# Experts ranked by token count on chip, the twelve emptiest run as six fp32 pairs, overflow only in a loop

## The chip, the cores and the metric

One core of a Trainium2 chip runs the whole program in one launch. The metric is the device time of that launch in microseconds. TensorE (PE) multiplies matrices, VectorE (DVE), ScalarE (ACT) and GpSimd (POOL) work element by element, SyncE (SP) mostly issues transfers, and 16 DMA engines move data. Each engine follows its own order of instructions and waits on semaphores for the others.

## The reference

Two layers over 1024 tokens of width 1024. Each has a mixer (layer 0 a state space scan, layer 1 dilated window attention) and then a mixture of 32 experts. The change touches the experts alone:

```python
def _hierarchical_moe(x, w_rg, b_rg, w_re, b_re, w_gate, w_up, w_down):
    ...
    g_w, g_idx = lax.top_k(jax.nn.softmax(g_logits, axis=-1), 1)      # one of 4 groups
    ...
    e_w, e_idx = lax.top_k(jax.nn.softmax(e_logits, axis=-1), MOE_TOP_K)  # 2 of its 8 experts
    e_w = e_w / jnp.sum(e_w, -1, keepdims=True)
    gates = (g_w * e_w).reshape(-1)
    ...
        h = jax.nn.silu(xb @ w_gate[e]) * (xb @ w_up[e])              # hidden width 512
        return h @ w_down[e]
    ...
    y = jax.ops.segment_sum(y_rows * row_gate[:, None], row_tok, num_segments=t + 1)[:t]
...
        x = _layer_norm(DEEPNORM_ALPHA * x + ffn, ln_g[i, 1], ln_b[i, 1])
```

Everything is float32. Each token goes to two experts, so a layer has 2048 assignments, 64 an expert on average. An expert's three matrices are 6 MB, and all 32 of them 192 MB a layer.

## The kernel before

**Tokens.** A router (class `Router`) works out gates and, for each expert, a column of token numbers `toks` with 112 places (`CAP`). Rows of x lie in the DRAM tensor X. `gather` (L924) brings an expert's rows into a buffer G by an indirect DMA on POOL's queue; places without a token are out of bounds and move nothing. `rows_out` (L997 to L999) copies the result to y and adds it to the DRAM tensor S with an indirect scatter. S starts as a copy of X (L1063) and holds the sum that the layer's norm reads at the end.

**Steps.** `Moe.run` walks 33 steps: the 32 experts in order, and a step 32 put in after the first 12 (`OVER`). That step takes the rows beyond 112 of the first expert that has too many; `overflow` (called at step 4) finds it, `place` lists its rows, and its weights are loaded only if there is one (`cond`). PE does that step either way. A loop at the very end takes further overflows, if any.

**Inside a step.** Step n does `up` for expert n (gate and up products into the PSUM tiles gu), the transposes of the next rows (L940), and `down` for expert n-1 (into dn), then the transposes of h. TensorE runs single-pass fp32r products, so weights and rows are split into a high part and a low rest, and every product is three matmuls (`mm3`, L175 to L177). ACT makes the high part wh (L916) and DVE the rest wl (L920) of each weight piece.

**Weights.** An expert's weights come in six pieces of 1 MB, four for gate and up and two for down. SP issues them in order (L900). They land in a ring of 10 buffers `wr`, and the first 14 pieces use four more buffers (`pre`). A buffer is free again once both splits have read it, so SP waits for the splits. The order of loads, splits, transposes and matmuls on each engine is as written in `Moe.run` (`chain`, `behind`); the rest follows from waits on tiles.

Of the kernel before, what the change touches and what calls it, by code (L numbers as in the profile page):

```python
# [21 lines left out]
P = 128  # L22
# [20 lines left out]
OVER = 12  # L43
# [7 lines left out]
OVT = 4  # L51
# [10 lines left out]
YB = 3  # L62
PLD = 6
# [579 lines left out]
class Router:  # L643
# [5 lines left out]
    def __init__(self, tc, cm, pool, keep, early, dram, layer, runs, w_rg, b_rg, w_re, b_re):  # L649
# [14 lines left out]
        self.X = dram.tile([T, D], F32, name=f"X{layer}")  # L664
        self.known = pool.tile([P, NT, 2, 2], F32, name=f"known{layer}")
# [11 lines left out]
    def tile(self, i, a, half, pt, pl):  # L677
# [4 lines left out]
        (nc.scalar if self.layer in XACT else nc.sync).dma_start(token_rows(self.X, self.runs[i], D), a)  # L682
# [147 lines left out]
    def overflow(self, pool, tmp, pp):  # L830

        nc, cm, V = self.nc, self.cm, self.nc.vector
        pc = pp([32, 2])
        nc.tensor.matmul(pc[:, 0:1], lhsT=self.total, rhs=cm.ones_b[:, 0:1], start=True, stop=True)
        ex, gt, M = tmp[:32, 0:1], tmp[:32, 64:64 + T // CAP], tmp[:32, 128:129 + 2 * OV]
        V.tensor_scalar(gt, cm.iota[0:32, 1:T // CAP + 1], float(CAP), None, op0=ALU.mult)
        V.tensor_tensor(gt, gt, pc[:, 0:1].to_broadcast([32, T // CAP]), op=ALU.is_lt)
        V.tensor_reduce(ex, gt, axis=AX.X, op=ALU.add)
        pc2 = pp([32, 2])
        nc.tensor.matmul(pc2[:, 0:1], lhsT=cm.triu[0:32, 0:32], rhs=ex, start=True, stop=True)  # L840
        V.tensor_tensor(M[:, 0:OV], cm.iota[0:32, 0:OV], pc2[:, 0:1].to_broadcast([32, OV]), op=ALU.is_ge)
        V.tensor_tensor(M[:, OV:2 * OV], M[:, 0:OV], ex.to_broadcast([32, OV]), op=ALU.mult)
        V.tensor_copy(M[:, 2 * OV:], ex)
        pr = pp([P, 2 * OV + 1])
        nc.tensor.matmul(pr, lhsT=cm.ones[0:32, :], rhs=M, start=True, stop=True)
        tab = pool.tile([P, OV + 2], I32, name="ov_tab", bufs=1)
        V.tensor_scalar(tab[:, 0:OV], pr[:, 0:OV], 31.0, None, op0=ALU.min)
        V.tensor_copy(tab[:, OV:OV + 1], pr[:, 2 * OV:])
        V.tensor_scalar(tab[:, OV + 1:], pr[:, 2 * OV:], 1.0, 0.0, op0=ALU.subtract, op1=ALU.max)

        base = pool.tile([P, OV], F32, name="ov_base", bufs=1)
        V.scalar_tensor_tensor(base, pr[:, OV:2 * OV], -1.0, cm.iota[:, 1:OV + 1], op0=ALU.mult, op1=ALU.add)
        V.tensor_scalar(base, base, float(CAP), None, op0=ALU.mult)
        V.scalar_tensor_tensor(base, pr[:, 0:OV], 1024.0, base, op0=ALU.mult, op1=ALU.add)
        return tab, base
# [8 lines left out]
class Moe:  # L864
# [6 lines left out]
    def run(self, extra=lambda tmp: None):  # L871
# [5 lines left out]
        dr = self.scope.enter_context(tc.tile_pool(name=f"m_dram{self.layer}", bufs=1, space=DRAM))  # L877
# [12 lines left out]
        self.S = S = dr.tile([T, D], F32, name="S")  # L890
# [4 lines left out]
        def raw(src, wr=None, **kw):  # L895
            wr = wr or spare()
            if kw:
                nc.gpsimd.memset(wr, 0.0)
            with behind(tc, *self.loads[-1:]):
                self.loads.append(nc.sync.dma_start(wr.rearrange("p (k n) -> p k n", n=src.shape[-1]), src, **kw))  # L900
            return wr
# [8 lines left out]
        def weights(src, wr, *gate):  # L910

            cnt[0] += 1
            n = src.shape[-1]
            wh = hp.tile([P, 2048], F32R, name="wh")
            wl = lp.tile([P, 2048], F32R, name="wl")
            chain("act", lambda: nc.scalar.activation(wh, wr, AF.Copy))  # L916
            if cnt[0] in PLO:
                nc.gpsimd.tensor_tensor(wl, wr, wh.bitcast(F32), op=ALU.subtract)
            else:
                chain("dve", lambda: nc.vector.tensor_tensor(wl, wr, wh.bitcast(F32), op=ALU.subtract), *gate)  # L920
            return [(wh[:, k:k + n], wl[:, k:k + n]) for k in range(0, 2048, n)]

        def gather(g, tok):
            return nc.gpsimd.indirect_dma_start(out=g[:CAP], out_offset=None, in_=rt.X[:, :],  # L924
                                         in_offset=bass.IndirectOffsetOnAxis(ap=tok[:CAP], axis=0),
                                         bounds_check=T - 1, oob_is_err=False)

        def parts(wg, wu, wd):

            up = [w.rearrange("(p k) n -> p k n", k=KD)[:, q:q + 4, :] for w in (wg, wu) for q in range(0, KD, 4)]  # L930
            down = [wd.rearrange("(k p) n -> p k n", p=P)[:, q:q + 2, :] for q in range(0, 4, 2)]
            return list(zip(up, [None] * len(up))), list(zip(down, [None] * len(down)))

        def flip(src, width):

            pts = []
            for q in range(0, width, 4):
                pts.append(ps.tile([P, 4, CAP], F32, name="tr"))
                for k in range(4):
                    make = lambda: nc.tensor.transpose(pts[-1][:, k, :], src[q + k], cm.ident[:CAP, :CAP])  # L940
# [4 lines left out]
        def parted(pts, name):  # L945
            h, l = [sp.tile([P, 4 * len(pts), CAP], F32R, name=name + x, bufs=XB) for x in "hl"]
# [6 lines left out]
        def rows_in(g):  # L953
            g = g[:CAP].rearrange("t (p k) -> t k p", k=KD)
            return parted(flip([g[:, k, :] for k in range(KD)], KD), "x")

        def up(x, pieces, between=lambda: None):

            xh, xl = x
            pg = [ps.tile([CAP, 512], F32, name="gu") for _ in range(2)]  # L960
            n = 0
            for j, (src, wr) in enumerate(pieces):
                for w in wr if isinstance(wr, list) else weights(src, wr):
                    i, kk = divmod(n, KD)
                    make = lambda: mm3(nc, pg[i], xh[:, kk, :], xl[:, kk, :], *w, kk == 0, kk == KD - 1)
                    last = make() if n else chain("pe", make)
                    n += 1
                if j == BETW:
                    between()
# [3 lines left out]
        def hidden(pg, gate):  # L973

            h = sp.tile([P, 512], F32, name="h")[:CAP]
            chain("act", lambda: nc.scalar.activation(h, pg[0], AF.Silu))
            chain("dve", lambda: nc.vector.scalar_tensor_tensor(h, h, gate[:CAP], pg[1], op0=ALU.mult, op1=ALU.mult))
            return h

        def hidden_in(h):  # L980
            return flip([h[:, k * P:(k + 1) * P] for k in range(4)], 4)

        def down(h, ws):
            hh, hl = h
            p = [ps.tile([CAP, 512], F32, name="dn", bufs=DB) for _ in range(2)]
            for kk, (wh, wl) in enumerate(ws):
                for n in range(2):
                    ns = slice(512 * n, 512 * n + 512)
                    make = lambda: mm3(nc, p[n], hh[:, kk, :], hl[:, kk, :], wh[:, ns], wl[:, ns], kk == 0, kk == 3)
                    last = make() if kk + n else chain("pe", make)  # L990
            self.last["pe"] = [last]
            return p

        def rows_out(p, tok):

            y = sp.tile([CAP, D], F32, name="y", bufs=YB)
            chain("act", lambda: nc.scalar.activation(y[:, 0:512], p[0], AF.Copy))  # L997
            chain("dve", lambda: nc.vector.tensor_copy(y[:, 512:1024], p[1]))
            nc.gpsimd.indirect_dma_start(out=S[:, :], out_offset=bass.IndirectOffsetOnAxis(ap=tok[:CAP], axis=0),  # L999
                                         in_=y, in_offset=None, bounds_check=T - 1, oob_is_err=False,  # L1000
                                         compute_op=ALU.add)

        def split_down(pieces):
            return [w for piece in pieces for w in weights(*piece)]
# [14 lines left out]
        def load(pieces, *slots, **kw):  # L1019
            for i in slots:  # L1020
# [26 lines left out]
        U, W, xs, hs, ps_dn = {}, {}, {}, {}, {}  # L1047
        U[0], W[0] = parts(w_gate[0], w_up[0], w_down[0])
        U[1], W[1] = parts(w_gate[1], w_up[1], w_down[1])
        U[2], W[2] = parts(w_gate[2], w_up[2], w_down[2])  # L1050
        U[3], W[3] = parts(w_gate[3], w_up[3], w_down[3])
        ahead = [(U[0], k) for k in range(4)] + [(p[e], k) for e in range(3) for p, e, n in ((U, e + 1, 4), (W, e, 2))
                                                 for k in range(n)]
# [5 lines left out]
        toks, known = rt.toks, rt.known_all  # L1059
        first = [gather(G[n], toks[:, n:n + 1]) for n in range(2)]  # L1060
# [7 lines left out]
        U[0][0] = (U[0][0][0], weights(*U[0][0], known))  # L1068

        order = [*range(OVER), 32, *range(OVER, 32)]  # L1070
        spots = {e: (toks[:, e:e + 1], rt.gates[:, e:e + 1]) for e in range(32)}
        kw = {e: {} for e in range(32)}
        for n in range(34):
            if n == OVT:
# [564 lines left out]
```

## Time and profile before

| | |
|---|---|
| median of 3 runs | 2935.34 us (2928.9 to 2938.06) |
| the profiled execution | 2933.27 us, span 2931.4 us |
| mean granted TensorE clock | 0.961 |
| busy, share of the span | PE 93%, DVE 75%, ACT 54%, POOL 24% |
| moved | 654.30 MB, mean 223 GB/s |
| experts, layer 0 | first gate product 893.18 us |
| wh split of a weight piece (L916) | 388 times, mean 1917 ns |
| wl split of a weight piece (L920) | 385 times, mean 2297 ns |

The profile's page cuts the span into 40 slices of some 73 us and gives for each the busy tenths of every engine, the granted clock and the DMA share. Lines of the trace read: start in us, length, engine, line of the kernel, operation, output, inputs. What stands in brackets at the end is the idle time before it and what ended it. A transfer's row gives the time of its issue on the queue; the time to its landing is given apart.

### The profile page before, as it was taken

How to read it: one execution, taken by the hardware profiler on the slowest of the kernel's cores; microseconds unless marked ns; L12 is line 12 of the kernel's file. 1: busy time of each engine (PE TensorE's matmuls, PEld its weight loads, DVE VectorE, ACT ScalarE, POOL GpSimd, SP SyncE). 2: the span in 40 equal slices, each digit the busy share in tenths (PEclk: the TensorE clock that was granted, in tenths of full speed). 3: DMA queues.
4: the chain of work that ended last, by engine and by line, in shares of the span. 5: the costliest groups of instructions: out<-in, count | busy, mean ns of one | idle time of the engine just before them, and what ended most of it. 6: DMA issues, size and time to landing. Idle time of an engine off the chain costs nothing. (4 is left out here: it accounts for less than half of the span.)

```text
span 2931.4 us, 45437 instructions
## 1 busy us (share of the span) xinstructions
PE 2739.0 (93%) x17068; PEld 2258.9 (77%) x17068; DVE 2204.7 (75%) x3730; ACT 1588.9 (54%) x2158; POOL 711.4 (24%) x589
## 2 busy tenths in 40 slices
PE   6999999999988999999969999999998999999992
PEld 5778878788766677777749999999977777777771
DVE  4677676897686899999966544655568889999886
ACT  3354442544425677777742444444442767777772
POOL 0044232334443232122211000111122224111224
PEclk8999999999998999999989999999987999999996
DMA  6455443645467998999965332333245999999994
GB/s 120 117 155 144 135 128 101 189 123 151 142 246 260 332 361 301 373 369 374 369 226 167 103 115 81 99 120 110 72 159 199 311 350 360 374 370 370 359 354 139
DMA packets 333269, 654.30 MB, mean 223 GB/s; under 512 B 35532, under 2 KB 236660, under 8 KB 299636
## 3 DMA queue, kind: packets, MB, share of 16 engines
q1 hardware_dynamic: 313268, 599.87, 58.4%
q0 software_dynamic: 17472, 43.08, 6.4%
q10 hardware_dynamic: 2304, 8.39, 0.7%
q8 instruction: 137, 2.24, 0.3%
q14 instruction: 88, 0.72, 0.1%
HBM read 624.49 MB, written 68.42 MB: 236 GB/s over the span
## 5 line engine op out<-in xcount | busy, mean ns | idle before, releaser
L920 DVE TENSOR_TENSOR wl<-wr,wh 128x2048 fp32r<-128x2048 f32 x385 | 883.7, 2297 | 125.4 <-PE gu L176 65.3
L916 ACT ACTIVATE wh<-wr 128x2048 fp32r<-128x2048 f32 x388 | 743.1, 1917 | 203.3 <-PE gu L177 133.6
L176 PE MATMUL gu<-wl,xh 128*112 128x512 f32 x1056 | 419.6, 397 | 12.6 <-DVE wl L920 9.4
L175 PE MATMUL gu<-wh,xh 128*112 128x512 f32 x1056 | 423.3, 402 | 2.0 <-ACT wh L916 2.0
L177 PE MATMUL gu<-wh,xl 128*112 128x512 f32 x1056 | 420.9, 399 | 0.0
L171 DVE TENSOR_TENSOR wl<-wr,wh 128x1024 fp32r<-128x1024 f32 (+1 forms) x146 | 229.8, 1574 | 165.4 <-ACT wh L170 163.8
L175 PE MATMUL mm<-wh,xh 128*128 128x256 f32 x1152 | 339.2, 295 | 0.5 <-ACT qk L1283 0.5
L176 PE MATMUL mm<-wl,xh 128*128 128x256 f32 x1152 | 330.0, 287 | 0.0
L177 PE MATMUL mm<-wh,xl 128*128 128x256 f32 x1152 | 329.4, 286 | 0.0
L170 ACT ACTIVATE wh<-wr 128x1024 fp32r<-128x1024 f32 (+1 forms) x146 | 186.4, 1277 | 214.7 <-PE mm L176 98.8
L924 POOL DMA_INDIRECT G<-X,toks x64 | 110.3, 1723 | 620.0 <-PE tr L940 588.5
L175 PE MATMUL mm<-xth,wh 128*128 128x512 f32 x640 | 255.1, 399 | 1.6 <-DVE carry L383 1.2
L176 PE MATMUL mm<-xtl,wh 128*128 128x512 f32 x640 | 253.5, 396 | 1.9 <-DVE xtl L171 1.9
L177 PE MATMUL mm<-xth,wl 128*128 128x512 f32 x640 | 254.5, 398 | 0.3 <-DVE wl L171 0.3
L176 PEld LDWEIGHTS gu<-wl,xh 128*112 128x112 f32 x1056 | 186.9, 177 | 77.4 <-DVE wl L920 14.3
L177 PEld LDWEIGHTS gu<-wh,xl 128*112 128x112 f32 x1056 | 186.0, 176 | 59.4 <-DVE xl L950 0.4
L175 PEld LDWEIGHTS gu<-wh,xh 128*112 128x112 f32 x1056 | 185.8, 176 | 59.2 <-ACT wh L916 2.4
L175 PEld LDWEIGHTS mm<-wh,xh 128*128 128x128 f32 x1152 | 220.8, 192 | 6.8 <-ACT qk L1283 1.0
L999 POOL DMA_INDIRECT S<-y,toks x64 | 147.8, 2309 | 318.5 <-DVE hl L950 143.7
L176 PEld LDWEIGHTS mm<-wl,xh 128*128 128x128 f32 x1152 | 221.2, 192 | 1.3
L177 PEld LDWEIGHTS mm<-wh,xl 128*128 128x128 f32 x1152 | 220.9, 192 | 0.4
L177 PE MATMUL dn<-wh,hl 128*112 128x512 f32 x528 | 209.3, 397 | 2.3 <-DVE hl L950 2.3
(409 smaller groups left out, 5410.8 us busy)
## 6 DMA issues: line engine op xcount, KB each, us to landing
wr<-in_moe_w_gate_dram SPq DMA_DIRECT2D x130, 1024.0 KB, 11.2
wr<-in_moe_w_down_dram SPq DMA_DIRECT2D x130, 1024.0 KB, 13.0
wr<-in_moe_w_up_dram SPq DMA_DIRECT2D x128, 1024.0 KB, 14.4
wr<-in_ssd_w_in_dram SPq DMA_DIRECT2D x80, 512.0 KB, 3.8
wr<-in_attn_w_qkv_dram SPq DMA_DIRECT2D x36, 1024.0 KB, 5.2
E<-csd SPq DMA_DIRECT2D x32, 512.0 KB, 4.2
wr<-in_ssd_w_out_dram SPq DMA_DIRECT2D x32, 512.0 KB, 4.0
xt<-x SPq DMA_DIRECT2D x24, 512.0 KB, 3.8
```

What stands on the lines that cost most here:

```text
L170: return (nc.scalar.activation(hi, src, AF.Copy), (eng or nc.vector).tensor_tensor(lo, src, hi.bitcast(F32), op=ALU.subtract))
L171: (eng or nc.vector).tensor_tensor(lo, src, hi.bitcast(F32), op=ALU.subtract))
L175: nc.tensor.matmul(out, lhsT=sh, rhs=mh, start=first, stop=False)
L176: nc.tensor.matmul(out, lhsT=sh, rhs=ml, start=False, stop=False)
L177: return nc.tensor.matmul(out, lhsT=sl, rhs=mh, start=False, stop=last)
L916: chain("act", lambda: nc.scalar.activation(wh, wr, AF.Copy))
L920: chain("dve", lambda: nc.vector.tensor_tensor(wl, wr, wh.bitcast(F32), op=ALU.subtract), *gate)
L924: return nc.gpsimd.indirect_dma_start(out=g[:CAP], out_offset=None, in_=rt.X[:, :], in_offset=bass.IndirectOffsetOnAxis(ap=tok[:CAP], axis=0),
L999: nc.gpsimd.indirect_dma_start(out=S[:, :], out_offset=bass.IndirectOffsetOnAxis(ap=tok[:CAP], axis=0), in_=y, in_offset=None, bounds_chec ...
```

## The change

Experts 0 to 3 stay as they are. `Router.plan`, called at step 1, counts the tokens of all experts on chip, ranks experts 4 to 31 by count, and gives a table of their numbers, their token columns and gates by rank. The rest of the layer runs 22 steps by rank. `S` is a single expert of 112 rows. `D` is the fullest one with a second block of 32 rows. `P` is a pair of the twelve emptiest: 64 rows of each on one half of the columns, multiplied as plain fp32 straight from the raw weight pieces (`product`), without splits. A pair uses one gather of 128 rows and two scatters, and 12 weight pieces. Weights of ranked experts are addressed by numbers that SP reads from the table. What doesn't fit any of this runs in the loop at the end only. S is no longer copied from X: the router writes each tile of rows to both. The PSUM tiles gu and dn share six buffers, ACT alone copies y out, y has two buffers instead of three.

```diff
+STEPS = "SSSS" "PSSPSDSPSSSPSSSPSSSSSP"
+ONES, PAIRS = 16, 6
+HALF = 64
+MORE = 32
+PLAN = 1
...
-YB = 3
-PLD = 6
+YB = 2
+PLD = 4
...
-        (nc.scalar if self.layer in XACT else nc.sync).dma_start(token_rows(self.X, self.runs[i], D), a)
+        for dst in (self.X, self.S):
+            (nc.scalar if self.layer in XACT else nc.sync).dma_start(token_rows(dst, self.runs[i], D), a)
...
-    def overflow(self, pool, tmp, pp):
+    def plan(self, pool, t, pp):
...
+        V.scalar_tensor_tensor(kb, pc[0:32], 32.0, iota, op0=ALU.mult, op1=ALU.subtract)
+        V.scalar_tensor_tensor(kc, cnt, 32.0, num, op0=ALU.mult, op1=ALU.subtract)
+        V.tensor_tensor(d[:, :n], kb[:, FIXED:], row(kc, n), op=ALU.is_gt)
+        V.tensor_reduce(rank, d[:, :n], axis=AX.X, op=ALU.add)
...
+        self.tokens(toks[:, :ONES + PAIRS], known[:, 0], t[:, 480:480 + ONES + PAIRS])
+        nc.gpsimd.memset(toks[0:HALF, ONES + PAIRS:], T)
+        V.tensor_copy(toks[HALF:, ONES + PAIRS:], toks[HALF:, ONES:ONES + PAIRS])
...
-                make = lambda: mm3(nc, pg[i], xh[:, kk, :], xl[:, kk, :], *w, kk == 0, kk == KD - 1)
...
+        def product(out, x, k, w, n, first, last):
+            if isinstance(x, list):
+                for z in range(2):
+                    c = slice(HALF * z, HALF * z + HALF)
+                    i = nc.tensor.matmul(out[c], lhsT=x[k][:, c], rhs=w[z][:, n], start=first, stop=last)
+                return i
+            (xh, xl), (wh, wl) = x, w
+            return mm3(nc, out, xh[:, k, :], xl[:, k, :], wh[:, n], wl[:, n], first, last)
+
+        def pick(st, slots):
+            return [w for _, w in slots] if st.two else slots[0][1] if isinstance(slots[0][1], tuple) else weights(slots[0][1])
...
+            pg = [[ps.tile([b.tok.shape[0], 512], F32, name="gu", tag="acc", bufs=6) for _ in range(2)] for b in st.blocks]
...
-            chain("dve", lambda: nc.vector.tensor_copy(y[:, 512:1024], p[1]))
...
+                for tok in ((b.tok[:HALF], b.second) if st.two else (b.tok,)):
+                    nc.gpsimd.indirect_dma_start(
+                        out=S[:, :], out_offset=bass.IndirectOffsetOnAxis(ap=tok, axis=0), in_=y[:tok.shape[0]],
+                        in_offset=None, bounds_check=T - 1, oob_is_err=False, compute_op=ALU.add)
...
-        for i in range(0, T, T // NS):
-            with behind(tc, *first):
-                nc.gpsimd.dma_start(S[i:i + T // NS, :], rt.X[i:i + T // NS, :])
...
-        order = [*range(OVER), 32, *range(OVER, 32)]
...
-                kw[32] = dict(cond=n_over > 0)
...
+            if n == PLAN:
+                plan = rt.plan(sp, sp.tile([P, 512], F32, name="h", bufs=2), lambda s: ps.tile(s, F32, name="tr"))
...
+                if n >= FIXED:
+                    st.U, st.W = parts(*(of_expert(nc.sync.value_load(tab[0:1, OV + 1 + r:OV + 2 + r], min_val=0, max_val=31))
+                                         for r in st.experts))
...
-        n_rest = nc.values_load(tab[0:1, OV + 1:OV + 2], min_val=0, max_val=OV - 1)
-        with tc.For_i(0, n_rest, 1) as v:
+        n_over = nc.values_load(tab[0:1, OV:OV + 1], min_val=0, max_val=OV)
+        with tc.For_i(0, n_over, 1) as v:
```

Step 4 on PE, layer 0. Before, a matmul of the overflow table (L845, into a tile tr) stands ahead of the transposes of the next rows and the down product of the expert before:

```order
L845 MATMUL tr<-pre_9385,ones 128x41
L940 MATMUL tr<-ident,G_8810 128x112 x8
L175 MATMUL dn<-wh,hh 112x512
L176 MATMUL dn<-wl,hh 112x512
L177 MATMUL dn<-wh,hl 112x512
```

After, step 4 is the first pair. Its gate and up products are two rows each for a half of the depth, straight from wr:

```order
L1008 MATMUL tr<-ident,h 128x112 x4
L1046 MATMUL gu<-wr,xh 64x512 x14
L1046 MATMUL gu<-wr,xl 64x512 x2
L1046 MATMUL gu<-wr,xh 64x512 x14
L1046 MATMUL gu<-wr,xl 64x512 x2
L1008 MATMUL tr<-ident,G_8816 128x112 x8
L181 MATMUL dn<-wh,hh 112x512
```

The pair takes 32 matmuls on 64 columns for gate and up, where two single experts take 2 x 48 on 112 columns.

SP, layer 0, the first weights after those loaded ahead. Before, the loads of the overflow table (`ov_tab`) stand among them once the first steps' weights are out:

```order
L900 DMA wr<-in_moe_w_up_dram 128x2048
L1104 DMA pre_9918<-in_ln_g_dram 128x1024
L1076 TENSOR_LOAD ov_tab
L1076 ISA x2
L1077 TENSOR_LOAD ov_tab
L1077 ISA x2
```

After, reads of expert numbers from the plan's table (`pl_tab`) come earlier and more often: four ahead of the last piece of the fixed experts shown here, and a further 14 like the last ones ahead of the first ranked piece:

```order
L968 DMA wr<-in_moe_w_up_dram 128x2048 x2
L968 DMA wr<-in_moe_w_down_dram 128x2x1024
L1240 TENSOR_LOAD pl_tab
L1240 ISA x2
L1240 TENSOR_LOAD pl_tab
L1240 ISA x2
L1240 TENSOR_LOAD pl_tab
L1240 ISA x2
L1240 TENSOR_LOAD pl_tab
L1240 ISA x2
L968 DMA wr<-in_moe_w_down_dram 128x2x1024
```

Weights now stand behind the plan on SP.

POOL, layer 0, start of the experts. Before, the copy of X to S follows the first two gathers of `toks`:

```order
L924 DMA G_8810<-X_236,toks_247 112x1024 x2
L1063 DMA S<-X_236 64x16384
L1207 MEMSET mask 128x256
L667 IOTA known_9560 128x2 x8
L673 MEMSET before_9572 128x32
L924 DMA G_8812<-X_236,toks_247 112x1024 x2
```

After, the copy is gone and the fifth gather, of 128 rows, already reads the plan's columns (`pl_toks`); the scatters follow in between:

```order
L890 MEMSET pl_toks 64x6
L992 DMA G_8816<-X_236,toks_248 112x1024 x2
L992 DMA G_8818<-X_236,toks_248 112x1024 x2
L985 TENSOR_TENSOR wl<-wr,wh 128x2048
L985 TENSOR_TENSOR wl<-pre_8825,wh 128x2048
L992 DMA G_8816<-X_236,pl_toks 128x1024
L992 DMA G_8816<-X_236,pl_toks 112x1024
L992 DMA G_8818<-X_236,pl_toks 112x1024
L1107 DMA S_237<-y,toks_248 1024x1024
```

The first gathers from the plan's columns now stand ahead of the first scatter, so POOL meets the plan before it adds any row to S.

More of the change, by code (lines that the diff above doesn't have):

```diff
@@ L50 @@
 OV = 20
-OVT = 4
+FIXED = 4
+STEPS = "SSSS" "PSSPSDSPSSSPSSSPSSSSSP"
[3 more added lines that the diff above has]
+PLAN = 1
 DB = 4
@@ new lines, in plan, with new, row @@
+        n, iota, eye = 32 - FIXED, cm.iota[0:32], cm.ident[0:32, 0:32]
+        at = [0]
+        def new(w):
+            at[0] += w
+            return t[:32, at[0] - w:at[0]]
+        def row(c, w):
+            return c.to_broadcast([32, w])
+        pc = pp([P, 32])
+        nc.tensor.matmul(pc, lhsT=cm.ones_b, rhs=self.total, start=True, stop=True)
+        aT = new(2 * P).rearrange("e (a p) -> e a p", a=2)
+        pa = pp([32, 2, P])
+        for k, a in enumerate((self.acc, self.gates)):
+            nc.tensor.transpose(pa[:, k, :], a, cm.ident)
@@ new lines, in plan @@
+        V.tensor_tensor(cap, cap, low, op=ALU.add)
+        V.tensor_tensor(cnt, cnt, cap, op=ALU.subtract)
+        gt = new(T // CAP)
+        V.tensor_scalar(gt, iota[:, 0:T // CAP], float(CAP), None, op0=ALU.mult)
+        V.tensor_tensor(gt, gt, row(cnt, T // CAP), op=ALU.is_lt)
+        V.tensor_reduce(ex, gt, axis=AX.X, op=ALU.add)
+        pe = pp([32, 2])
+        nc.tensor.matmul(pe[:, 0:1], lhsT=cm.triu[0:32, 0:32], rhs=ex, start=True, stop=True)
+        end = kc
+        V.tensor_copy(end, pe[:, 0:1])
@@ L951, in parted, with whole @@
             return h, l
[L953 to L964, printed above, removed]
-                    make = lambda: mm3(nc, pg[i], xh[:, kk, :], xl[:, kk, :], *w, kk == 0, kk == KD - 1)
-                    last = make() if n else chain("pe", make)
-                    n += 1
+        def whole(pts, name):
+            n = 4 * len(pts)
+            h, l = [sp.tile([P, n, CAP], F32R, name=name + x, bufs=XB).bitcast(F32).rearrange("p k t -> p (k t)") for x in "hl"]
+            to = h[:, 0:P * (n - 1)].rearrange("p (k t) -> p k t", t=P)
+            for q, pt in enumerate(pts):
+                m = min(4, n - 1 - 4 * q)
+                chain("act", lambda: nc.scalar.activation(to[:, 4 * q:4 * q + m], pt[:, 0:m], AF.Copy))
+                if m < 4:
+                    chain("dve", lambda: nc.vector.tensor_copy(l[:, 0:P], pt[:, 3]))
+            return [to[:, k] for k in range(n - 1)] + [l[:, 0:P]]
@@ new lines, in pick, with by, up @@
+        def pick(st, slots):
+            return [w for _, w in slots] if st.two else slots[0][1] if isinstance(slots[0][1], tuple) else weights(slots[0][1])
+        def by(st, slots):
+            n = 1 + st.two
+            return [slots[i:i + n] for i in range(0, len(slots), n)]
+        def up(st, between=lambda: None):
+            pg = [[ps.tile([b.tok.shape[0], 512], F32, name="gu", tag="acc", bufs=6) for _ in range(2)] for b in st.blocks]
+            for j, slots in enumerate(by(st, st.U)):
+                ws = pick(st, slots)
+                for q in range(4):
+                    i, kk = divmod(4 * j + q, KD)
+                    for x, p in zip(st.x, pg):
+                        make = lambda: product(p[i], x, kk, [w[:, 512 * q:512 * q + 512] for w in ws], slice(None), kk == 0,
+                                               kk == KD - 1)
+                        last = make() if j + q or p is not pg[0] else chain("pe", make)
@@ L1003, in split_down, with down @@
-        def split_down(pieces):
-            return [w for piece in pieces for w in weights(*piece)]
+            return flip([h[:, k * P:(k + 1) * P] for k in range(4)], 4, h.shape[0])
+        def down(st, ws):
+            out = []
+            for b, h in zip(st.blocks, st.h):
+                p = [ps.tile([b.tok.shape[0], 512], F32, name="dn", tag="acc", bufs=6) for _ in range(2)]
+                for kk in range(4):
+                    w = [w[:, 1024 * (kk % 2):1024 * (kk % 2) + 1024] for w in ws[kk // 2]]
+                    for n in range(2):
+                        make = lambda: product(p[n], h, kk, w, slice(512 * n, 512 * n + 512), kk == 0, kk == 3)
+                        last = make() if kk + n else chain("pe", make)
+                self.last["pe"] = [last]
+                out.append(p)
+            return out
@@ L1006, in pair, with split_down @@
+        def split_down(st):
+            return [pick(st, slots) for slots in by(st, st.W)]
         def pair(i):
@@ L1019, in load @@
         def load(pieces, *slots, **kw):
-            for i in slots:
+            for i in slots or [i for i in range(len(pieces)) if pieces[i][1] is None]:
                 pieces[i] = (pieces[i][0], raw(pieces[i][0], **kw))
@@ L1045, in of_expert, with __init__ @@
             return [w[bass.ds(e, 1)].rearrange("o a b -> (o a) b") for w in (w_gate, w_up, w_down)]
[L1047 to L1053, printed above, removed]
+        class Step:
+            def __init__(self, blocks, two=False):
+                self.blocks, self.two = blocks, two
+        class Block:
+            def __init__(self, tok, gate):
+                self.tok, self.gate = tok, gate
+        toks, known = rt.toks, rt.known_all
+        steps = [Step([Block(toks[:CAP, e:e + 1], rt.gates[:CAP, e:e + 1])]) for e in range(FIXED)]
+        for e, st in enumerate(steps):
+            st.U, st.W = parts([w[e] for w in (w_gate, w_up, w_down)])
+        ahead = [(steps[0].U, k) for k in range(4)]
+        ahead += [(p, k) for e in range(FIXED - 1) for p, n in ((steps[e + 1].U, 4), (steps[e].W, 2)) for k in range(n)]
         ahead = ahead[:len(SLOTS[self.layer])]
@@ L1058, in run, with gathers @@
             load(p, k, wr=slot)
-        toks, known = rt.toks, rt.known_all
-        first = [gather(G[n], toks[:, n:n + 1]) for n in range(2)]
-        for i in range(0, T, T // NS):
-            with behind(tc, *first):
-                nc.gpsimd.dma_start(S[i:i + T // NS, :], rt.X[i:i + T // NS, :])
+        blocks, n_in = [], [0]
+        def gathers(upto):
+            while n_in[0] < min(upto, len(blocks)):
+                b, k = blocks[n_in[0]], n_in[0]
+                b.g = G[k % 4]
+                first.append(gather(b.g, b.tok))
+                n_in[0] += 1
+        blocks += [st.blocks[0] for st in steps]
+        first = []
+        gathers(2)
+        first = first[:2]
         for (p, k), slot in zip(ahead[late:], slots[late:]):
@@ new lines, in more @@
+        def more(plan):
+            ptoks, pgates, tab, base = plan
+            one, two = iter(range(1, ONES)), iter(range(PAIRS))
+            for kind in STEPS[FIXED:]:
+                if kind == "P":
+                    q = next(two)
+                    c = slice(ONES + q, ONES + q + 1)
+                    st = Step([Block(ptoks[:, c], pgates[:, c])], True)
+                    st.experts = ONES + q, ONES + PAIRS + q
+                    st.blocks[0].second = ptoks[:, ONES + PAIRS + q:ONES + PAIRS + q + 1]
+                else:
+                    r = next(one) if kind == "S" else 0
+                    st = Step([Block(ptoks[:CAP, r:r + 1], pgates[:CAP, r:r + 1])])
+                    st.experts = r,
+                    if kind == "D":
+                        st.blocks.append(Block(None, None))
+                steps.append(st)
+                blocks.extend(st.blocks)
@@ new lines, in run @@
+        N = len(STEPS)
+        for n in range(N + 1):
+            st = steps[n] if n < N else None
+            before = steps[n - 1] if n else None
+            if n == PLAN:
+                plan = rt.plan(sp, sp.tile([P, 512], F32, name="h", bufs=2), lambda s: ps.tile(s, F32, name="tr"))
+                tab, base = plan[2:]
+                more(plan)
+            if n == STEPS.index("D") - PLD:
+                tok, gate = place(slice(OV, OV + 1), kp.tile([P, 2048], F32, name="pre3"), "tok1")
+                d = steps[STEPS.index("D")].blocks[1]
+                d.tok, d.gate = tok[:MORE], gate[:MORE]
```

211 lines of the change are left out of this document (110 added, 101 removed).

## The prediction

> **What bounds the kernel now.** I read the 40 slices of the page first, then windows over the two MoE phases, the chain that ended last, the landing times of the weight transfers, and single rows for prices.
>
> ```profile
> PE   6999999999988999999969999999998999999992
> PEclk8999999999998999999989999999987999999996
> DMA  6455443645467998999965332333245999999994
> GB/s 120 117 155 144 135 128 101 189 123 151 142 246 260 332 361 301 373 369 374 369 226 167 103 115 81 99 120 110 72 159 199 311 350 360 374 370 370 359 354 139
> ```
>
> TensorE is busy almost everywhere. Transfers are only near full in the two MoE phases (about 890 to 1510 us and 2260 to 2880 us), where they reach 369 to 374 GB/s and no more. The windows put both beside each other. Their columns are the window, its length, the busy time of PE, PEld, DVE, ACT and POOL with counts, the granted clock, the DMA share and GB/s:
>
> ```profile
> 893.00:961.00 68.00, 62.63 (x273) 46.71 (x272) 51.38 (x35) 47.95 (x38) 22.28 (x8) 0.95 0.82 265
> 961.00:1000.00 39.00, 33.56 (x148) 24.87 (x147) 32.12 (x50) 24.57 (x21) 6.86 (x5) 0.94 0.97 356
> 1150.00:1475.00 325.00, 325.00 (x1521) 249.91 (x1520) 296.65 (x200) 251.18 (x200) 63.22 (x34) 1.00 1.01 371
> 2400.00:2700.00 300.00, 300.00 (x1404) 230.72 (x1403) 273.91 (x184) 232.14 (x184) 73.24 (x38) 1.00 1.01 369
> 2700.00:2860.00 160.00, 156.53 (x721) 117.74 (x720) 140.76 (x97) 118.09 (x95) 34.32 (x16) 1.00 0.98 353
> ```
>
> In the long middle of each layer PE is never idle and the DMA engines are full at the same time. The chain says which of them sets the end (start, length, what):
>
> ```profile
> 2446.21 0.88 PE tr L940 x8
> ...
> 2464.18 0.88 PE tr L940 x8
> ...
> 2685.88 25.00 DMA wr<-in_moe_w_down_dram
> ...
> 2760.38 27.13 DMA wr<-in_moe_w_down_dram
> ...
> 2874.34 5.84 DMA S<-y,toks
> ...
> 2880.95 6.14 DMA S<-y,toks
> ...
> 2888.04 3.62 DMA pre<-S
> ```
>
> Up to about 2686 us the path is PE, one step every 2464.18 - 2446.21 = 17.97 us. Then layer 1 hands over to the weight transfers, and ends in two scatters and the reading of S. So PE is a hair ahead of the transfers as the limit, and the transfers are already losing ground. How fast they lose it is in the landing times of the line that issues weights, for pieces issued in 1150 to 1200, 1440 to 1476, 2500 to 2530 and 2660 to 2690 us:
>
> ```profile
> DMA to landing us min/median/max: 6.9/8.2/8.9
> ...
> DMA to landing us min/median/max: 21.8/23.2/25.1
> ...
> DMA to landing us min/median/max: 12.0/14.6/16.1
> ...
> DMA to landing us min/median/max: 20.2/22.4/25.0
> ```
>
> A step uses six 1 MB pieces, so they are issued every 17.97 / 6 = 2.995 us. In layer 0 the landing time grows by 15.0 us over the 283 us between the middles of the windows, in layer 1 by 7.8 us over 160. A piece is therefore served in 2.995 x (1 + 15.0/283) = 3.15 us, or 2.995 x (1 + 7.8/160) = 3.14. I take 3.15, which is 18.9 us per expert against PE's 17.97. The issuing queue waits for free slots, not the reverse:
>
> ```profile
> SPq L900 <- DVE wl L920: 800.5, 295, 22.0
> ```
>
> **Where the count starts.** The first four experts are untouched. Step 4 starts at the first two rows, and the last weight split at the last two:
>
> ```profile
> 968.93 0.47 PE L175 MATMUL gu<-wh,xh 128*112 128x512 f32 x1
> ...
> 2336.86 0.47 PE L175 MATMUL gu<-wh,xh 128*112 128x512 f32 x1
> ...
> 1498.46 1.92 ACT L916 ACTIVATE wh<-wr 128x2048 fp32r<-128x2048 f32 x1 [0.86 <-DVE h L977]
> ...
> 2868.35 1.92 ACT L916 ACTIVATE wh<-wr 128x2048 fp32r<-128x2048 f32 x1 [1.11 <-DMA wr<-in_moe_w_down_dram]
> ```
>
> Weights issued in layer 0 from 810 to 969 us:
>
> ```profile
> L900 SPq DMA_DIRECT2D wr<-in_moe_w_gate_dram x10: 327/340/345, 814.2 to 958.9; - x10
> L900 SPq DMA_DIRECT2D wr<-in_moe_w_up_dram x10: 327/328/368, 828.9 to 964.5; - x10
> L900 SPq DMA_DIRECT2D wr<-in_moe_w_down_dram x9: 378/379/413, 845.9 to 968.4; - x9
> L900 SPq DMA_DIRECT2D pre<-in_moe_w_gate_dram x2: 328/334/341, 843.3 to 866.7; - x2
> L900 SPq DMA_DIRECT2D pre<-in_moe_w_up_dram x2: 382/383/384, 843.7 to 871.9; - x2
> ...
> DMA to landing us min/median/max: 4.8/5.9/12.2
> ```
>
> That is 33 pieces, 24 of them for the first four experts, so 9 are ahead; at 6 to 9 us from issue to landing some 3 of these are in flight. In front of step 4 stand 6 x 28 = 168 pieces, of which 168 - 9 + 3 = 162 are still to be served. The rate can be tested on layer 1 of this kernel, where the overflow step loads six more: 168 x 3.15 = 529, and 2336.9 + 529 = 2866 us, against 2868.35 measured. So there the transfers set the end. In layer 0 (no overflow load) they would be done at 968.9 + 162 x 3.15 = 1479, and PE, at 29 steps, ends it at 1498.
>
> **The change: PE.** From step 4 on there were 29 steps (28 experts and the overflow step, which PE runs in both layers): 29 x 17.97 = 521 us. Now there are 15 single steps, one double step and 6 pairs. A pair multiplies raw fp32 weights, two experts on two column halves. No row shows this at 512 columns; the nearest are:
>
> ```profile
> 216.51 1.02 PE L540 MATMUL st<-xrd,Bt 128*128 128x512 f32 x2
> ...
> 196.12 1.09 PE L548 MATMUL yd<-E,xr 128*64 128x128 f32 x16
> ...
> 1703.03 0.69 PE L1467 MATMUL pv<-vt,pT 128*64 128x64 f32 x16
> ```
>
> A plain fp32 product of 512 columns is two passes; the two records of 0.59 us in 1.02 us start 0.43 apart, so it occupies PE for 0.86. yd and pv are eight products each on 64-column halves. One after the other, yd would be 16 passes x 0.43 x 128/512 = 1.72 us, and it takes 1.09; in twos side by side it would be 0.86 and a tail. So halves run together, and I price a pair of products at 0.87 (lower end; upper end 1.72, one after the other). A pair has 16 such for gate and up and 8 for down: 24 x 0.87 + 1.26 for twelve transposes = 22.2 us, against 2 x 17.97. The double step's second block has only 32 rows but streams the same 512 columns, so it costs a whole step: 36. Sum: 6 x 22.2 + 15 x 17.97 + 36 = 439 us, 82 less than 521. PE stops being the limit. The splits that pairs save on ACT (1.92 us, row above) and DVE I count at nothing: neither engine ends a wait in the long windows.
>
> **Transfers.** The bytes of the 28 experts stay. What falls is the number of gathers and scatters, and the overflow expert's six pieces in layer 1. Their price comes from two pieces issued when no rows moved:
>
> ```profile
> L900 SPq DMA_DIRECT2D wr<-in_moe_w_gate_dram x2: 433/452/470, 2206.9 to 2207.4; - x2
> ...
> DMA to landing us min/median/max: 6.9/8.0/9.0
> ```
>
> They landed at 2213.8 and 2216.4: 2.6 us a piece (371 GB/s would make it 1.0486/371 = 2.83). An expert's rows then cost (3.15 - 2.6) x 6 = 3.3 us. A pair moves its rows with one gather and two scatters; between one expert's cost and two, 3.3 to 6.6, I take 5, the middle, as neither end is nearer. Pair: 12 x 2.6 + 5 = 36.2. Single: 18.9. Double: 15.6 + 4.3 (32 more rows) = 19.9. Sum: 6 x 36.2 + 15 x 18.9 + 19.9 = 521 us for 168 pieces, 3.10 each (3.04 with 3.3, 3.17 with 6.6). The remaining 162 take 502 us (492 to 513), which is above PE's 439.
>
> A rule of the Trainium skill ("Perfetto Trace Analysis", Roofline) allows one active core some 435 GB/s through its 16 DMA engines; by it the 502 would shrink to 502 x 371/435 = 428, below PE. The trace's flat top of 369 to 374 at a share of 1.01 speaks for the smaller limit.
>
> **The start, the queues, the end.** The plan now stands at step 1, with some 33 small DVE operations, and its token columns must reach POOL before the gather for step 4. Before, the overflow table stood at step 4 and cost this:
>
> ```profile
> 984.73 0.77 PE L940 MATMUL tr<-ident,G 112*128 112x112 f32 x4 [2.87 <-DVE xl L950]
> 985.73 0.63 PE L176 MATMUL dn<-wl,hh 128*112 128x512 f32 x1
> ...
> DMA to landing us min/median/max: 16.4/17.0/17.6
> ...
> L1077 SPq TENSOR_LOAD <-ov_tab x2: 271/272/272, 992.4 to 2352.8; - x2
> ```
>
> A wait of 2.87 us and slow matmuls after it, together about 5. The plan delays splits queued behind it on DVE, and through them slots and the weights on SP: 5 again. Each of the 28 expert numbers costs SP a load and register work, about half a microsecond (fourth row), and 18 stand in a row between two weight pieces of the first steps: some 9 us without an issue. Slots are what SP waits for then too, but with 6 us from issue to landing the engines run dry for about 3. I add 5 + 3 = 8 us before step 4 (0 if both hide, 15 if neither does). The copy of X to S on POOL (third row, 17 us to land just as the weights are wanted) goes; eight more row writes on ACT's queue, spread over the time before, take its place. I count both at nothing, since DMA is far from full there. SP's other index loads hide under its 800 us of waits for slots.
>
> At the end the last down product needs no split, but its rows go out in two scatters in series instead of one: 6.1 us more by the row at 2880.95, some 3.6 less for PE and DVE: +2.5 a layer. The loop at the end runs no times, as before.
>
> **Sum.** Layer 0: last piece at 968.9 + 8 + 502 = 1479 against 1498.5, -19.5. Layer 1: 2336.9 + 8 + 502 = 2847 against 2868.3, -21.5. With +2.5 twice: -36. The profiled run took 2933.3 in all, 2.1 under the median of 2935.3; -36 on the median gives 2899.
>
> **Rivals.** (A) The forecast, bound by transfers. Its own bounds: 3.04 and 3.17 us a piece (10 or 11 either way a layer), the start 0 to 15 (8 either way). Taken as independent, 13 a layer: 2873 to 2925.
>
> (B) Within 0.3% (about 9 us, what a measurement can tell from no change): a pair needs 12 pieces and the ring has 10 slots; its raw slots are held until both halves are multiplied. If each pair leaves the transfers without free slots for 3 us, that is 6 x 3 = 18 a layer, 2935. Against it: at 1150 us the DMA share was 1.01 with a landing time of 8.2 us, so under three pieces in flight kept the engines full.
>
> (C) The clock. PE will wait at pairs, 439 of 502 us busy, 87%. The rows at 893 and 961 us, busy 92% and 86%, show 0.95 and 0.94, and at 0.94 PE needs 467, still hidden. It decides below 439/520 = 0.84, where the whole gain of 18 a layer is gone; at 0.75 PE needs 585, 83 over, 3065. Speaking for it: after the 2.87 us wait a matmul took 0.63 us (row at 985.73), against 0.47 for one at the start of step 4. The Trainium skill ("TensorE: Matmul & The Clock Gate", Part 1, HAM oscillation) describes this very pattern, short bursts of matmuls with 3 to 5 us waits on DMA, as running at half clock; the trace has seen the slowing, not yet a loop that stays in it.
>
> (D) The change doesn't do what it says: halves run one after the other. A pair is then 24 x 1.72 + 1.3 = 42.6, PE's sum 6 x 42.6 + 270 + 36 = 562, 41 more than before instead of 82 less; with the ends about +45 a layer, 3025. The yd row stands against it.
>
> (E) More is gained. If rows cost next to nothing and weights go at 2.83: 162 x 2.83 = 458, 44 a layer less, 2811. If transfers are no limit at all, PE decides: -82 a layer, 2771. The handover to weight transfers at 2686 us in the chain is against both.
>
> **Chances.** A 0.63, B 0.13, C 0.09, D 0.04, E 0.11. All of A and E is faster (0.74), B is the same (0.13), C and D slower (0.13). From 2850, which takes in the nearer part of E, to 2943, the upper end of B, leaves out C, D and half of E, some 0.18.
>
> **What would show it.** Right: in the MoE phases DMA at 1.00 and 360 to 375 GB/s from step 4 on; PE idle some 60 us a layer, released by weights; the steps of pairs about 36 us apart though their matmuls fill 22; the last weights at about 1479 and 2847 us. Wrong: matmuls on halves at starts 0.43 us apart for each half (D), a granted clock under 0.85 in the phase (C), a DMA share under 0.95 with SP waiting for PE (B), or GB/s well over 374 (E).

## The result and the profile after

The change takes the kernel to 2856.72 us (median of 4 runs, 2851.93 to 2862.64), from 2934.7 us (4 runs): ratio 0.9737, 95% interval 0.9712 to 0.9762. The forecast was 2899. The direction held, and the transfers took PE's place as the limit, but the gain is 78 us where 36 were forecast. Times are medians of fast runs; of the four executions with the plan a step later, one took 13471.62 us and is left out, and why it did is open.

The profiled execution, the slowest of the four, took 2862.64 us, with a span of 2860.8. Its 40 slices:

```profile
PE   6999999999987999989968999999999899999892
PEclk8999999999997999999989999999997899999996
DMA  6454443645465899999965332332336599999994
GB/s 123 111 168 142 122 147 104 204 129 149 128 212 213 297 398 381 364 388 373 394 237 204 108 116 72 105 123 89 99 111 265 183 367 384 362 393 391 380 372 151
```

The flat top of 369 to 374 GB/s is gone. The slices now reach 398 and 394. So the old top was not the most that the transfers can reach. Windows of after, from step 4 to the last down product of each layer, and of before below (columns as in the prediction):

```profile
978.00:1477.00 499.00, 466.62 (x2161) 291.42 (x2158) 273.05 (x205) 253.96 (x239) 84.41 (x47) 0.98 0.98 370
2313.00:2805.00 492.00, 467.49 (x2159) 293.39 (x2157) 269.87 (x187) 253.73 (x237) 86.23 (x47) 0.97 0.98 372
```

```profile
969.00:1509.00 540.00, 532.78 (x2523) 408.19 (x2521) 485.34 (x360) 403.96 (x321) 121.90 (x61) 0.99 0.95 343
2337.00:2879.00 542.00, 533.65 (x2522) 406.41 (x2521) 481.83 (x339) 402.44 (x319) 122.75 (x60) 1.00 0.97 351
```

PE's share falls from 99% to 94 or 95%, DVE's work by 44%. The mean DMA share over the phase rises to 0.98, though much the same weights are moved. The first pair starts at the first row, and the first products of the two layers at the next two (before: 893.18 and 2260.71):

```profile
978.32 6.23 PE L1046 MATMUL gu<-wr,xh 128*64 128x512 f32 x28
...
893.58 0.77 PE L181 MATMUL gu<-wh,xh 128*112 128x512 f32 x1
...
2228.46 0.77 PE L181 MATMUL gu<-wh,xh 128*112 128x512 f32 x1
```

The first row has 28 records, seven pairs of products of two passes each, in 6.23 us: 14 steps of 0.43 and a tail. The halves run side by side, as priced. The end of the chain, start, length and what (the view follows it back no further than 2798 us, so it doesn't say what held the steps before):

```profile
2798.11 1.46 DMA S<-y,pl_toks
...
2810.99 4.61 DMA S<-y,pl_toks
...
2818.89 6.62 DMA pre<-S
```

### The profile page after: what moved, and what is told of

It reads as the page before. It is cut to its first block, busy times and chain, and to the rows that moved or that the text cites. A ratio compares the mean times of both kernels' runs of the same rounds, so it can differ in the third digit from the quotient of the medians.

```text
span 2860.8 us, 43810 instructions
## 1 busy us (share of the span) xinstructions
PE 2617.6 (91%) x16376; PEld 2034.6 (71%) x16376; DVE 1792.5 (63%) x3504; ACT 1286.5 (45%) x1998; POOL 640.4 (22%) x565
## 5 line engine op out<-in xcount | busy, mean ns | idle before, releaser
L987 DVE TENSOR_TENSOR wl<-wr,wh 128x2048 fp32r<-128x2048 f32 x229 | 526.4, 2304 | 292.9 <-ACT wh L983 214.6
L983 ACT ACTIVATE wh<-wr 128x2048 fp32r<-128x2048 f32 x232 | 443.5, 1916 | 281.3 <-DMA wr<-in_moe_w_down_dram 108.7
L182 PE MATMUL gu<-wl,xh 128*112 128x512 f32 x640 | 258.3, 404 | 23.7 <-DVE wl L987 20.0
L181 PE MATMUL gu<-wh,xh 128*112 128x512 f32 x640 | 259.5, 407 | 2.7 <-ACT wh L983 2.6
L183 PE MATMUL gu<-wh,xl 128*112 128x512 f32 x640 | 257.8, 403 | 0.0
L1107 POOL DMA_INDIRECT S<-y,pl_toks x56 | 105.2, 1879 | 340.1 <-ACT y L1105 240.3
L1046 PE MATMUL gu<-wr,xh 128*64 128x512 f32 x672 | 157.9, 596 | 9.4 <-DMA wr<-in_moe_w_up_dram 8.7
L182 PEld LDWEIGHTS gu<-wl,xh 128*112 128x112 f32 x640 | 114.4, 179 | 69.1 <-DVE wl L987 28.8
L182 PE MATMUL dn<-wl,hh 128*112 128x512 f32 x320 | 133.7, 418 | 16.3 <-DVE wl L987 16.2
L181 PEld LDWEIGHTS gu<-wh,xh 128*112 128x112 f32 x640 | 114.3, 179 | 42.0 <-ACT wh L983 4.6
```

The lines of the kernel that those rows point to most:

```text
L181: nc.tensor.matmul(out, lhsT=sh, rhs=mh, start=first, stop=False)
L182: nc.tensor.matmul(out, lhsT=sh, rhs=ml, start=False, stop=False)
L183: return nc.tensor.matmul(out, lhsT=sl, rhs=mh, start=False, stop=last)
L1046: i = nc.tensor.matmul(out[c], lhsT=x[k][:, c], rhs=w[z][:, n], start=first, stop=last)
```

## The experiments

Each is timed against the kernel before on the same chip, where that kernel's median lies between 2932.25 and 2934.97 us. "Transfers" below is the time from the start of step 4 to the landing of the last weight piece, layers 0 and 1, worked out from the trace's completion records. It is 529.2 and 531.3 us before, 492.4 and 485.5 after. The forecast said 502.

**Address order and registers.** Four theories stood for the missing 42 us: ADDRESS, REGISTER, SPLITS and ROWS. The first kernel puts the ranked order into the kernel before (RANKED stands for the two lists of numbers that are written out there):

```diff
-        order = [*range(OVER), 32, *range(OVER, 32)]
+        seq = [0, 1, 2, 3] + RANKED[self.layer]
+        order = [*seq[:OVER], 32, *seq[OVER:]]
```

> The kernel before, with experts 4 to 31 walked in the order that the change gives on these inputs (fixed numbers, written into the program). Nothing else is changed. Theory ADDRESS (jumping between experts in DRAM lets weight transfers run faster): landing times of weights no longer grow to 22 to 25 us in the long windows, layer 1 no longer ends on weights, total some 10 us less, about 2925. Theories REGISTER (addresses from a register are faster), SPLITS (fewer splits disturb transfers less) and ROWS (a pair's gather and scatters cost less than I took): no change, 2935.

Measured 2932.6 us, ratio 1.000 (0.9986 to 1.0014). Pieces issued in 1440 to 1476 us still land after 23.5 us (22.0 to 24.7). The other three change the addresses in the kernel after. For fixed addresses in natural order (in ranked order the list is that of the ranks; with registers the reads stay, and the table holds 4 to 31):

```diff
-                    st.U, st.W = parts(*(of_expert(nc.sync.value_load(tab[0:1, OV + 1 + r:OV + 2 + r], min_val=0, max_val=31))
-                                         for r in st.experts))
+        self.nat = list(range(FIXED, 32))
...
+                    es, self.nat = self.nat[:len(st.experts)], self.nat[len(st.experts):]
+                    st.U, st.W = parts(*([w[e] for w in (w_gate, w_up, w_down)] for e in es))
```

> The kernel after, but weights of experts 4 to 31 are loaded in their natural order at fixed addresses, with no expert number read by SP; tokens stay by rank, so each token meets another expert's weights. Same work otherwise. ADDRESS and REGISTER: weight transfers fall back to 3.10 us a piece or more, +18 us a layer, about 2893. SPLITS and ROWS: no change, 2857. If the 28 reads of numbers on SP cost time, 5 to 10 us less than that.

> The kernel after with addresses from registers as they are, but the table holds the experts in natural order; tokens stay by rank, so each token meets another expert's weights. ADDRESS: about 2893. REGISTER, SPLITS, ROWS: 2857.

> The kernel after with the same ranked order, but at fixed addresses (the order of these inputs written into the program), with no number read by SP. REGISTER: about 2893. ADDRESS, SPLITS, ROWS: 2857, or 5 to 10 us less if the reads on SP cost time.

Measured 2859.35, 2858.7 and 2856.57 us. ADDRESS and REGISTER fall. And the 28 reads on SP cost nothing that shows: without them (ranked order) step 4 starts 85.9 and 84.8 us after the layer's first product, with them 84.7 in both layers.

**Only the pairs undone.**

```diff
-STEPS = "SSSS" "PSSPSDSPSSSPSSSPSSSSSP"
-ONES, PAIRS = 16, 6
+STEPS = "SSSS" "SSSSSD" + "S" * 22
+ONES, PAIRS = 28, 0
```

> The kernel after without pairs: the ranking, the plan, the double step and the missing copy stay, but all other ranked experts are single steps (27 of them and the double step). By the prediction's sum PE has 29 steps of 17.97 from step 4 on as before, 521 us, and the plan adds 8 us a layer: about 2950. If any of the gain comes from the other parts of the change (no copy of X to S, ranked order), it is below 2930. Theory SPLITS (splits on ACT and DVE slow the packets of weight transfers): the transfers run as in the kernel before, at most 371 GB/s. Theory LAYOUT (other places of buffers in memory): they stay above 380 where they are full.

Measured 2934.9 us, ratio 1.000 (0.9988 to 1.0011): without the pairs nothing is left of the gain. That is a balance: the plan's cost is there, as step 4 starts 86.0 and 83.9 us after the first product (75.8 and 76.2 in the kernel before), but from there to the last down product the layers take 535.3 and 534.6 us instead of 540.0 and 541.8. So the other parts of the change win back most of the plan's cost; which of them is open. Transfers run no faster than before, which rules out LAYOUT:

```profile
1150.00:1440.00 290.00, 290.00 (x1357) 222.64 (x1357) 256.67 (x163) 231.68 (x194) 54.45 (x32) 1.00 1.02 368
```

**The splits that pairs save.** Put back, with results that nobody reads:

```diff
+            if st.two:
+                for _, w in slots:
+                    weights(w)
```

> The kernel after, but each of a pair's 12 weight pieces is split on ACT and DVE as a single expert's pieces are, into buffers that nobody reads; PE multiplies raw weights as before. SPLITS: transfers fall back to 3.10 us a piece, +18 us a layer, about 2893. ROWS and LAYOUT: no change, 2857.

> As the run with splits nobody reads, but with DVE's operation alone (it reads the raw piece twice), nothing on ACT. SPLITS by DVE: about 2893; by ACT: 2857; by both alike: 2875.

Measured 2888.53 us (ratio 0.985, 0.9825 to 0.9876), and 2871.63 (0.9789, 0.9762 to 0.9817) with DVE's half alone. So the splits, which the prediction counted at nothing, are worth 32 us, about half of which comes with DVE's alone; ACT's alone was not run. The windows with both halves put back, over the same phase as above:

```profile
972.00:1488.00 516.00, 472.00 (x2159) 295.07 (x2157) 429.11 (x277) 381.68 (x310) 119.83 (x48) 0.95 0.95 358
2324.00:2830.00 506.00, 465.81 (x2158) 291.92 (x2158) 425.37 (x258) 379.61 (x307) 112.21 (x47) 0.97 0.96 362
```

DVE is busy 83% or 84% of the time, not all of it, and yet the DMA share drops from 0.98 to 0.95 and 0.96. Transfers take 503.0 and 494.4 us (+10.6, +8.9), and from the last landing to the last down product 12.6 and 11.5 us instead of 6.2 and 6.0. Together that is 31.4 us, about the whole cost. (The profiled executions differ by 25.1 us only, as this one reaches its first gate product 6.2 us earlier, before any pair runs.) Where buffers wait is in the queue's waits, of the kernel after and below it with the splits put back:

```profile
SPq L968 <- DVE wl L987: 303.5, 116, 19.1
...
SPq L968 <- PE gu L1046: 132.8, 43, 13.3
```

```profile
SPq L968 <- DVE wl L987: 481.9, 194, 19.1
```

Before, SP waited 800.5 us for DVE's split. A raw piece is freed by PE alone. With the splits back, SP waits longer for DVE, so buffers come free later. But this is not the only way in which they cost time. PE itself waits, here in layer 0 of the kernel after (978 to 1477 us), and below it with the splits put back (972 to 1488):

```profile
PE gu L182 <- DVE wl L987: 9.7, 9, 1.8
PE dn L182 <- DVE wl L987: 8.7, 6, 1.6
PE gu L1046 <- DMA wr<-in_moe_w_up_dram: 5.5, 5, 1.4
```

```profile
PE dn L182 <- DVE wl L987: 13.9, 6, 4.2
PE tr L1008 <- DVE xl L1018: 10.6, 3, 6.9
...
PE gu L1046 <- DMA wr<-in_moe_w_up_dram: 2.9, 2, 1.6
```

All of PE's waits for DVE and ACT in these windows grow from 26.1 to 41.1 us (layer 1: 21.1 to 38.6), while its waits for landing weights shrink. So what PE needs from DVE and ACT also comes later with the idle splits among their work. How the 32 us divide between late buffers and late operands, the run does not show.

**The rows of the pairs.** Their gathers and scatters are left out:

```diff
-                first.append(gather(b.g, b.tok))
+                if not hasattr(b, "second"):
+                    first.append(gather(b.g, b.tok))
...
-                for tok in ((b.tok[:HALF], b.second) if st.two else (b.tok,)):
+                for tok in (() if st.two else (b.tok,)):
```

> The kernel after without the gathers and scatters of the pairs (their rows are neither read nor added). By the prediction a pair's rows cost 5 us of transfers: -30 us a layer, about 2797, unless PE's 439 stops it earlier. Theory ROWS (they cost 1 to 2 us): -6 to -12 a layer, 2833 to 2845.

Measured 2813.87 us (ratio 0.959, 0.9567 to 0.9614), 43 less than the kernel after and between the two forecasts. Transfers take 479.6 and 476.4 us, 12.8 and 9.1 less, so 1.8 us a pair where I took 5; of the rest, 20 lie after the last down products, which no scatter follows then. The 1.8 is a lower bound, since PE is close to its own limit there, 464 of 484 us:

```profile
982.00:1466.00 484.00, 463.78 (x2157) 290.23 (x2156) 272.95 (x205) 253.93 (x238) 63.06 (x33) 0.98 0.98 373
```

**Where the rows of a single lie.** The price of 3.15 us a piece came from landing times, and a piece has landed when the last of 16 engines is done. The completion records of all 16 show what that hides. The table gives the median time in us from the issue of a piece until the first, 4th, 8th, 12th and last engine was done with it, for pieces issued in 1300 to 1440 us:

```
before              5.4   5.7   7.6  16.1  19.9
after               6.0   6.5  15.6  16.9  23.1
before, dealt       5.2   5.7   6.1   6.8   8.1
after, dealt       14.1  17.1  18.3  20.0  21.6
```

Before, some eight engines are done with a piece within 7.6 us, while the last four need 16 us and more. The busy share of 1.01 counted all of them as full. The theory BALANCE blames the places of the rows: tokens fill an expert's 112 places from 0 up. The test deals them in strides, in the router's table:

```diff
-                    V.tensor_tensor(oc, cm.iotap, self.key[:, k, i0 + i:i0 + i + 1].to_broadcast([P, P]),
-                                    op=ALU.is_equal)
+                    kc = self.key[:, k, i0 + i:i0 + i + 1]
+                    V.tensor_tensor(oc[:, 0:112].rearrange("p (r q) -> p r q", q=7),
+                                    cm.iotap[:, 0:112].rearrange("p (q r) -> p r q", r=16),
+                                    kc[:, :, None].to_broadcast([P, 16, 7]), op=ALU.is_equal)
+                    V.tensor_tensor(oc[:, 112:P], cm.iotap[:, 112:P], kc.to_broadcast([P, 16]), op=ALU.is_equal)
```

> The kernel before, with each expert's tokens dealt over its 112 places in strides of seven (token j at place 7 (j mod 16) + j div 16) instead of from place 0 up, so that the empty places lie between them. Theory BALANCE (a gather or scatter deals its 112 rows to the 16 DMA engines in blocks of seven, so with 64 tokens some 9 engines carry all rows and fall behind, while the others wait for the next piece): the landing times no longer grow to 22 to 25 us but stay near 8 to 12, and layer 1 no longer ends on weights; PE at 17.97 us a step still sets the time, so 2925 to 2933. Without BALANCE: landing times grow as before, no change.

Measured 2927.69 us, ratio 0.9976 (0.9966 to 0.9986). The third line of the table shows all engines done within 8.1 us: the backlog is gone with the same rows and weights, so it came from the places of the rows. Layer 1 no longer ends on weights; its chain has PE's steps to the end (17.97 us apart, the last transposes of rows at 2847.28), then the scatters:

```profile
2847.28 0.88 PE tr L943 x8
2853.73 0.39 PE tr L943 x4
...
2874.28 5.55 DMA S<-y,toks
```

In the kernel after, the tokens of pairs are dealt over their 64 places as well:

> The kernel after with the tokens of singles and of pairs dealt evenly over their places in the same way. BALANCE: the transfers get past 383 GB/s and a piece down to about 2.9 us, some 12 us a layer less, about 2833. Without BALANCE: no change, 2857.

Measured 2833.84 us, ratio 0.9662 (0.9639 to 0.9685): faster than both kernels, by 23 us than the one after. Transfers take 474.9 and 472.4 us. The engines now lag more alike (last line of the table: 14.1 to 21.6 us from first to last, where it was 6.0 to 23.1), and they move more: after, and below it the dealt one, over the same window.

```profile
1000.00:1440.00 440.00, 411.48 (x1898) 265.18 (x1896) 252.99 (x175) 233.84 (x215) 78.74 (x43) 0.98 1.00 382
```

```profile
1000.00:1440.00 440.00, 420.47 (x1930) 265.88 (x1928) 251.92 (x171) 235.63 (x218) 77.75 (x44) 1.00 1.02 391
```

**The plan a step later** (`PLAN = 2`, on top of the dealt tokens):

> The same with the plan at step 2 instead of step 1, to see what the plan costs where it stands: if the 8 us before step 4 are its place, up to 5 us a layer less than the run with the plan at step 1; if its work only moves, the same; if the gather for step 4 then comes late, a few us more.

Measured 2841.28 us (three runs, 2838.01 to 2843.97), ratio 0.969 (0.9671 to 0.9709), some 7 above the run with the plan at step 1; as the intervals overlap, that it is slower is likely and not settled. Step 4 starts 86.6 and 86.7 us after the first product instead of 85.1 and 84.8, so the plan's cost moves along and gets no smaller. In the profiled executions most of the rest is in layer 0, where the transfers take 481.4 us instead of 474.9; why is open.

**The copy of X to S put back:**

```diff
-            for dst in (self.X, self.S):
+            for dst in (self.X,):
...
+        with behind(tc, *first):
+            nc.gpsimd.dma_start(S[:, :], rt.X[:, :])
```

> The kernel after with the copy of X to S put back on POOL's queue (as before the change) and the router writing X alone. The prediction counted the copy at nothing: 2857. If its 8 MB of reading and writing cost the start of each layer its 17 us in part, 2862 to 2880.

Measured 2865.28 us, ratio 0.9764 (0.9745 to 0.9784), against 0.9737 (0.9712 to 0.9762) for the kernel after. The intervals overlap. A cost of some 8 us is likely and not settled; in the trace neither step 4 (84.7 and 84.8 us) nor the transfers (492.1 and 484.2) are later. The 4 us between the profiled executions lie ahead of the first gate product of layer 0 (897.94 against 893.58 us), a time that varies from 887.42 to 899.59 over the runs here.

## Why the prediction was wrong

The terms of its sum, in us, against the profiled executions (times of the trace; "end" is from the last landing to the last down product, "after it" what follows):

| | forecast, layer 0 and 1 | measured |
|---|---|---|
| start of step 4 | +8, +8 | +9.0, +8.5 |
| transfers from there | 502 (-27, -29) | 492.4, 485.5 (-36.8, -45.8) |
| end | -3.6, -3.6 | -4.7, -4.4 |
| after it, second scatter | +6.1, +6.1 | -0.1, +3.2 |
| sum | -36 | -71 |

The medians differ by 78: the profiled execution of the kernel after is 6 us above its median, that of the kernel before 1 us below.

- **Right:** the pair on PE (side by side, 0.86 a product), the transfers as the new limit (waits of SP that an earlier weight transfer ended rise from 134.0 to 297.4 us, and dealing the rows, which spares PE and the splits nothing, takes off another 23), the start of step 4 in its size (but all of it the plan: the reads on SP, 3 of the 8, cost nothing that shows; they stand as 4 and 14 with a piece between, and the longer stretch without an issue is 8.6 us), the clock (0.97 and 0.98, with no wait of PE above 2.1 us in these windows, so rival C did not come). PE's 439 was low by some 20: 458.8 us busy in the dealt kernel. It did not matter yet.
- **Wrong, "the splits that pairs save on ACT and DVE I count at nothing":** this is the step that failed. They are worth 32 us, of which the sum had at most 7 (under "end"). I had looked at who waits inside PE's windows, and not at who frees the buffers, though the row of SP's 800.5 us of waits for the split stood in the prediction.
- **Wrong, the price of rows:** 18.9 us for a single and 5 for a pair's rows came from the most loaded engines of a stream of singles. The same stream needs no more than PE's 17.97 when rows are dealt evenly. For a pair the runs show 1.8 us or somewhat more. That its 128 places, filled in two blocks, spread the rows better than 112 places filled from one side is argued, not shown.
- **Wrong, the flat top of 369 to 374 GB/s as the limit:** 391 GB/s were moved over 440 us. I took the top of the trace for a limit; it was that of a set of engines of which half were done early, at a busy share of 1.01. The 435 GB/s of the Trainium skill ("Perfetto Trace Analysis", Roofline) were not reached here either: the highest slice of any run is 404.
- **Wrong, the second scatter:** +12 in the sum, +3 measured. In layer 0 nothing of it shows.
- **A slip in the sum:** with 6.6 us for a pair's rows a piece comes to 3.16 us, not 3.17, and the upper bound of the transfers to 511, not 513.
- **The signs:** PE was idle 32 and 25 us a layer, not 60, and the GB/s well over 374 that the prediction names as a sign of rival E came. That 2857 still lies between 2850 and 2943 is owed to the part of E in that range; A's own bounds, 2873 to 2925, miss it.

In numbers, transfers account for 26 of the 35 us between -36 and -71, the second scatter for 9, the end for 2, the start for -1.5. By the run with splits put back, the splits account for some 20 of the 26. That the transfers then take 503.0 us in layer 0, next to the 502 of the forecast, does not bear out its price of rows: there SP waits 194.3 us for DVE's split and 88.3 for earlier weight transfers, where in the kernel after it is 76.5 and 165.8, so other limits give the same time by luck. The rest of the 26 is open; the price of rows and the limit of 374 GB/s both point that way, and no run parts them.

## What to carry to other kernels

Before an operation is counted at nothing, ask what its end releases: a split that seems to end no wait of PE may still hold the buffer for which the next transfer waits, and delay the work behind it on its engine. Read a landing time as the slowest of 16 engines: here the first were done after 5 us while the last drifted to 20, and it was the placement of rows, with the same bytes, that brought the last down to 8. A busy share of 1.00 did not prove that the engines were used up: 371 GB/s went through at 1.01 in the kernel before, and 391 at 1.02 in the kernel after with its rows dealt.

## What was not expected of the hardware

The DMA share stood at 1.01 in windows in which about half of the engines finished each piece 5 to 8 us after its issue, and it stayed at 1.00 to 1.02 while the rate rose from 371 to 391 GB/s. In the full windows of both layers, 8 KB packets of weights took 340 ns on average in the kernel before (1150 to 1475 and 2400 to 2700 us) and 325 in the kernel after (1000 to 1440 and 2330 to 2660), with medians of 309 and 313: some packets are booked far longer (99th percentile 963 against 495 ns). Why is open. Uneven rows alone are not the reason: in the kernel before with its rows dealt, the same windows show 336 on average and a 99th percentile of 833. Which places of a gather go to which engine the records don't name; that blocks of seven places share an engine is argued from the effect of the stride.
